# Row-block order for the last piece of the first values, early copies of half products, and two smaller moves in a two-layer hybrid trunk

## The chip, the cores and the metric

The kernel runs on one core of one Trainium2 chip. The metric is the device time of one execution in microseconds. It is the median of three runs for the kernel before, and a profile of one further execution stands beside it.

## The reference

The model has two layers of width 1024 over a sequence of 512 positions, in float32. In short:

```python
# even layer
q, k, v, g_ret, xb, g_lru = jnp.split(x @ w_in, ...)          # six blocks of 1024 columns
ret = group_norm(retention(rope(q), rope(k) * dk**-0.5, v)) * silu(g_ret)   # 8 heads of 128
lru = rg_lru_branch(xb, ...) * silu(g_lru)                    # conv, gates, scan
h = layer_norm(alpha * x + concat(ret, lru) @ w_out)
# odd layer
q, k, v, g = jnp.split(h @ w_in, ...)                         # four blocks of 2048 columns
p = softmax(mask(rope(q) @ rope(k).T)); w = p[:, :, 0] - lam * p[:, :, 1]   # two maps a head, 8 heads
o = rms_norm(w @ v) * subln_g * (1 - lambda_init)
out = layer_norm(alpha * h + (o * silu(g)) @ w_out)
```

The group norm of the retention takes the mean over a head's 128 columns away; the kernel takes it away from the values v instead, ahead of the retention, which is linear in them.

## The kernel before, in words

**Products.** Every float32 operand is split into a high and a low half (`split`, L150 to L153: a cast to the high half, L152, mostly on ScalarE; a subtraction for the low half, L153, on VectorE). A product is three matmuls, high by high, low by high and high by low (`mm3`, L157). Nearly all of TensorE's work is such groups of three matmuls with 512 columns.

**Weights.** They come in 162 pieces of 128 x 1024 floats (512 KB). `fetch` (L177) loads a piece into a raw buffer by SyncE's queue, casts it, splits it, and appends it to the ready list; `take(ahead)` hands out the next piece and fetches a given number of pieces ahead of use. In a name like w3h the number is the piece's and the letter the half; the raw buffer is w_r. At the start there are two raw buffers, later four. The first piece, w0, is loaded, cast and split in two halves of 512 columns, between the loads of x's columns (xr).

**Order.** TensorE and SyncE run in the order in which the program is written. The other engines' order is made by a scheduler from priorities (`tc.high_priority`), and instructions given to `tc.keep_in_program_order` keep the written order among themselves. Work that belongs to attention, retention and so on is interleaved with the projections by a clock of ticks (`Side`): one tick is one group of three matmuls. A job such as `attention` yields the number of ticks after which its next step is due; tables at the head of the file hold these numbers. `ATT_TURN` is, for each of the four query blocks of a head, the ticks between the transposes of the weights of the softmax (L675, split into w..h and w..l) and their product with the values (po).

**First values.** `s_unit` computes the values of the first four heads, 512 columns, for four blocks of 128 rows into four PSUM banks (ev_ps). Each of the four pieces w0 to w3 covers two of the eight slices of the contraction. In this first unit of the program the matmuls go kind by kind over the four row blocks, as the condition on `taken[0]` says; elsewhere a piece goes row block by row block. `evac` in `v_even` then takes the mean per head (vm, L459 and L460) and subtracts it (vc, L462) on VectorE, and splits the result (ev00 to ev03). The next product (gl, from piece w4) takes the first bank that comes free.

**Gates and values of the odd layer.** Groups 1 to 3 of the heads have their gate and value projections computed together in `gates_values` (gv1 to gv3), by fewer products of sums of blocks. Two products share two banks each: `one` (gv1a, two banks) and `two` (gv1b). Between the products, partial results are copied out by ScalarE (L804, p1, u and p7), since the banks go on accumulating. `product` takes two pieces, and the callback `then` runs between them. The copies of one pair of banks are issued in the callback of the product of the other pair. `load_sum` (L775) loads sums of activations that a product further on reads.

**Attention.** For a head hd and a query block qb the job does the scores of the two maps (as), the exponentials (e, L663), the combination (L671), the transposes, the product with the values (po), the root mean square (L696, then GpSimd's L699 and L367), the scaling by the gate (o, L702), two more transposes (L706) and the split into the output operand (om). The last head, 7, ends together with the last output projection (oo_ps): its sums into y (L264) and the statistics of the final layer norm (L268, L377 to L396) are on VectorE.

Of the kernel before, what the change touches and what calls it, by code (L numbers as in the profile page):

```python
# [17 lines left out]
KT = D // P  # L18
# [13 lines left out]
LN_TURN = 15  # L32
ATT_START, ATT_GAP = (12,) * 7 + (7,), (8,) * 7 + (7,)
ATT_SCORES = (7, 7, 7, 9)
ATT_TURN = (4, 3, 4, 5)
ATT_NORM = 5
ATT_VALUE, GV_VALUE = 2, 4
ATT_FREE, ATT_LENT = 2, 8
# [65 lines left out]
def trunk(ctx: ExitStack, tc: tile.TileContext, a):  # L104
# [3 lines left out]
    def pool(name, bufs, stack=ctx, **kw):  # L108
        return stack.enter_context(tc.tile_pool(name=name, bufs=bufs, **kw))
# [18 lines left out]
    def work(name):  # L128
        return wk.tile([P, S], F32, tag="wk", name=name)
# [4 lines left out]
    def bank(pl, tag, name):  # L134
        return pl.tile([P, 512], F32, tag=tag, name=name)

    def pair(pl, shape, tag, name, **kw):
        return tuple(pl.tile(shape, F32R, tag=tag + x, name=name + x, **kw) for x in "hl")
# [4 lines left out]
    def cut(t, *ix):  # L143
        return t[0][ix], t[1][ix]

    def split(src, dst, scale=None, copy=nc.scalar.copy):
        if scale is not None:
            s = sg[:, scale:scale + 1]
            nc.scalar.activation(out=dst[0], in_=src, func=AF.Identity, scale=s)
            nc.vector.scalar_tensor_tensor(out=dst[1], in0=src, scalar=s, in1=dst[0].bitcast(F32), op0=ALU.mult, op1=ALU.subtract)  # L150
            return
        copy(out=dst[0], in_=src)  # L152
        return nc.vector.tensor_tensor(out=dst[1], in0=src, in1=dst[0].bitcast(F32), op=ALU.subtract)  # L153

    def mm3(out, l, r, start, stop, kinds=range(3), **kw):
        for n in kinds:
            nc.tensor.matmul(out=out, lhsT=l[n == 2], rhs=r[n == 1], start=start and n == 0, stop=stop and n == 2, **kw)  # L157
# [30 lines left out]
    taken = [0]  # L188

    def take(ahead):  # L190
        taken[0] += 1
        while len(ready) < min(taken[0] + ahead, len(order)):
            list(fetch())
        return ready[taken[0] - 1]
# [9 lines left out]
    def s_unit(act, name, major, evac, before=None):  # L204
        def product(ps, w, sb, kt, kinds=range(3)):
            j = kt % 2 * HALF
            mm3(ps, cut(act, ALL, kt, slice(sb * P, sb * P + P)), cut(w, ALL, slice(j, j + HALF)), kt == 0, kt == KT - 1, kinds)
            if 2 in kinds:
                if kt == KT - 1:
                    evac(sb, ps)  # L210
                side.tick()

        if major:
            with tc.high_priority(P_WEIGHTS):
                ws = [take(0) for _ in range(KT // 2)]
            for sb in range(SB):
                before(sb)
                ps = bank(ps_pj, "pj", f"{name}_ps{sb}")
                for kt in range(KT):
                    product(ps, ws[kt // 2], sb, kt)  # L220
        else:
            ps = [bank(ps_pj, "pj", f"{name}_ps{sb}") for sb in range(SB)]
            for i in range(KT // 2):
                w = take(2)
                if taken[0] <= KT // 2:

                    for j in range(2):
                        for n in range(3):
                            for sb in range(SB):
                                product(ps[sb], w, sb, 2 * i + j, (n,))  # L230
                    continue
                for sb in range(SB):
                    for j in range(2):
                        product(ps[sb], w, sb, 2 * i + j)
# [39 lines left out]
    for p in range(3):  # L274
        one, two = (2 * p, 2 * p + 1)
# [5 lines left out]
    for kind, i in ev:  # L281
        if kind in ("ro", "lo", "out"):
            order += [(eo[2 * i + j + n], None) for n in {"ro": (0,), "lo": (8,), "out": (8, 0)}[kind] for j in range(2)]
        else:
            n = 4 if kind == "v" else 1
# [45 lines left out]
    for n, (lo, hi) in enumerate(((0, 1), (1, 2), (2, 4), (4, 6), (6, 8))):  # L331
        nc.sync.dma_start(out=xr[:, lo:hi], in_=a["xt"][:, lo:hi])
        if n == 0:
            next(halves)
        for kt in range(lo, hi):
            low = split(xr[:, kt], cut(x, ALL, kt))
            if n == 0:
                tc.keep_in_program_order(low)
        if n == 1:
            list(halves)  # L340
        elif 1 < n < 4:
            list(fetch())
# [66 lines left out]
    two = pool("two", 2, phase)  # L409
# [240 lines left out]
    def attention(hd, qb, q, k, m):  # L650
# [25 lines left out]
        with tc.high_priority(P_ATT):  # L676
            wt = part(n, f"w{hd}{qb}")
            split(pt[:, :n], wt)
        yield ATT_TURN[qb] + busy[0]

# [92 lines left out]
    def load_sum(n, k):  # L773
        for j in range(2):
            nc.sync.dma_start(out=sx[:, k, :, 2 * j:2 * j + 2].bitcast(F32), in_=sd[n][:, :, 2 * j:2 * j + 2])  # L775

    def silu2(x, out, t):

        nc.scalar.activation(out=t, in_=x, func=AF.Tanh, scale=0.5)
        nc.vector.scalar_tensor_tensor(out=out, in0=t, scalar=1.0, in1=x, op0=ALU.add, op1=ALU.mult)  # L780

    def gates_values(i):
        def block(r, c):
            return lambda kt, n: cut(h, ALL, 4 * c + kt, slice((2 * r + n) * P, (2 * r + n) * P + P))

        def total(k):
            return lambda kt, n: tuple(sx[:, k, x, kt, n * P:n * P + P] for x in range(2))

        def product(ps, left, start, then=lambda: None):
            for j in range(2):  # L790
                if j:
                    then()
                w = take(3)
                for n in range(2):
                    for kt in range(2 * j, 2 * j + 2):
                        c = kt % 2 * HALF
                        mm3(ps[n], left(kt, n), cut(w, ALL, slice(c, c + HALF)), start and kt == 0, kt == KT // 2 - 1, skip_group_check=not start)
                        side.tick()

        def copies(ps, name, ts):  # L800

            for n in range(2):
                ts.append(work(f"{name}{i}{n}"))
                tc.keep_in_program_order(nc.scalar.copy(out=ts[n], in_=ps[n]))  # L804

        def gate(ps, ts, r):
            g = gp.tile([P, 2, S], F32, tag="g", name=f"og{i}{r}")
            for n in range(2):
                for hd in (2 * i - 2, 2 * i - 1):
                    side.need(oj[hd, 2 * r + n])  # L810
                gates[2 * r + n, i] = g[:, n]
            for n in range(2):
                nc.vector.tensor_tensor(out=g[:, n], in0=ps[n], in1=ts[n], op=ALU.add)
                silu2(g[:, n], g[:, n], ts[n])

        busy[0] = ATT_BUSY
        one = [bank(ps_pj, "pj", f"gv{i}a{n}") for n in range(2)]
        two = [bank(ps_pj, "pj", f"gv{i}b{n}") for n in range(2)]
        p1, u, p7, low = [], [], [], []
        product(one, block(0, 0), True)  # L820
        product(two, block(0, 1), True, lambda: copies(one, "p1", p1))
        gate(two, p1, 0)
        product(one, total(0), False)

        def between():
            load_sum(0, 0)
            copies(one, "u", u)

        product(two, total(1), True, between)

        def between():
            load_sum(3, 1)
            copies(two, "p7", p7)

        product(one, total(0), False, between)
        past(i - 1)
        for n in range(2):
            nc.vector.scalar_tensor_tensor(out=p7[n], in0=one[n], scalar=-1.0, in1=p7[n], op0=ALU.mult, op1=ALU.subtract)
            low.append(pair(vp, [P, S], "v", f"ov{i}{2 + n}"))
            split(p7[n], low[n])  # L840
        product(two, block(1, 1), False)
        gate(two, u, 1)
        product(one, total(1), False)
        for n in range(2):
            t = pair(vp, [P, S], "v", f"ov{i}{n}")
            nc.scalar.activation(out=t[0], in_=one[n], func=AF.Identity, scale=-1.0)
            nc.vector.scalar_tensor_tensor(out=t[1], in0=one[n], scalar=-1.0, in1=t[0].bitcast(F32), op0=ALU.mult, op1=ALU.subtract)
            vs.setdefault(i, []).append(t)
        vs[i] += low
        vt[i] = side.now + GV_VALUE  # L850
        busy[0] = 0
# [5 lines left out]
    def past(g):  # L857
        if g >= 0:
            for hd in (2 * g, 2 * g + 1):
                for qb in range(SB):  # L860
                    side.need(oj[hd, qb])
# [25 lines left out]
    for kind, i in od:  # L887
        spare[0] = kind == "qk"
        if kind == "v":
            vs[i] = []  # L890

            def evac(sb, ps):
                past(i - 1)
                t = pair(vp, [P, S], "v", f"ov{i}{sb}")
                split(ps, t)
                vs[i].append(t)

            s_unit(h, f"ov{i}", i == 0, evac, lambda sb: side.need(hj[sb]))
            vt[i] = side.now + ATT_VALUE
            if i == 0:  # L900
# [117 lines left out]
```

## Time and profile before

| | |
|---|---|
| median of 3 runs | 927.86 us |
| lowest and highest run | 926.43 and 928.98 us |
| profiled execution | 926.57 us |
| its span | 924.8 us |
| outside the span | 1.77 us |
| granted clock of TensorE | 0.998 |
| matmuls | 4256 |

Lines of the timeline read: start in us, length in us, engine, line of the kernel, operation, output, inputs, count, and in brackets the engine's idle time ahead of it with what released it. An x4 behind a line stands for four instructions, and the length is from the first start to the last end. PE is TensorE, DVE VectorE, ACT ScalarE, POOL GpSimd, SPq the queue of SyncE.

### The profile page before, as it was taken

How to read it: one execution, taken by the hardware profiler on the slowest of the kernel's cores; microseconds unless marked ns; L12 is line 12 of the kernel's file. 1: busy time of each engine (PE TensorE's matmuls, PEld its weight loads, DVE VectorE, ACT ScalarE, POOL GpSimd, SP SyncE). 2: the span in 40 equal slices, each digit the busy share in tenths (PEclk: the TensorE clock that was granted, in tenths of full speed). 3: DMA queues.
4: the chain of work that ended last, by engine and by line, in shares of the span. 5: the costliest groups of instructions: out<-in, count | busy, mean ns of one | idle time of the engine just before them, and what ended most of it. 6: DMA issues, size and time to landing. Idle time of an engine off the chain costs nothing.

```text
span 924.8 us, 11834 instructions
## 1 busy us (share of the span) xinstructions
PE 907.2 (98%) x4256; PEld 750.4 (81%) x4256; DVE 740.8 (80%) x1223; ACT 478.3 (52%) x779; POOL 114.9 (12%) x190
## 2 busy tenths in 40 slices
PE   9899999999999999999999999999999999999996
PEld 6788887888888888888888778888888888788885
DVE  5777977967868998897888887759877679868777
ACT  5466886637565668533434456433456333655340
POOL 1311010110102010010101120000120100201022
PEclk9999999999999999999999999999999999999999
DMA  7895363782829471434941216646237392268102
GB/s 258 279 289 165 108 184 107 219 226 57 254 62 287 115 195 58 168 128 148 330 171 69 69 68 222 226 167 233 77 129 256 148 317 79 75 240 285 53 1 91
DMA packets 46522, 152.92 MB, mean 165 GB/s; under 512 B 6144, under 2 KB 6272, under 8 KB 45696
## 3 DMA queue, kind: packets, MB, share of 16 engines
q1 hardware_dynamic: 41472, 135.39, 41.5%
q0 software_dynamic: 4992, 16.78, 9.3%
q8 instruction: 33, 0.54, 0.2%
q14 instruction: 25, 0.20, 0.1%
HBM read 139.57 MB, written 37.75 MB: 192 GB/s over the span
## 4 chain that ended last, share of the span: by engine, by line
PE 84%; DVE 7%; ACT 3%; DMA 2%; issue 2%; POOL 1%; SPq 0%; DVEq 0%; ACTq 0%; POOLq 0%
PE oo_ps L157 7%; PE gr_ps L157 5%; PE out_ps L157 4%; PE q_ps L157 4%; PE gl_ps L157 4%; PE k_ps L157 4%; PE xb_ps L157 4%; PE po L157 3%; PE as L157 3%; PE gv2a L157 2%; PE ov_ps L157 2%; PE gv3a L157 2%; PE ev_ps L157 2%; PE eo_ps L157 2%; PE og_ps L157 2%; DMA w_r<-in_ev_w 2%
## 5 line engine op out<-in xcount | busy, mean ns | idle before, releaser
L663 ACT ACTIVATE e<-as,nm 128x128 f32<-128x128 f32 (+3 forms) x64 | 33.2, 523 | 61.2 <-DVE nm L660 61.1
L670 POOL TENSOR_SCALAR zr<-z 128x1 f32<-128x1 f32 x32 | 16.9, 528 | 246.9 <-ACT e L663 246.9
L702 DVE SCALAR_TENSOR_TENSOR o<-po,ars,og 128x256 f32<-128x256 f32 x32 | 15.5, 484 | 33.2 <-POOL ars L367 33.2
L185 POOL DMA_DIRECT2D t<-t x24 | 18.8, 783 | 159.3 <-DMA t<-in_od_w 155.4
L699 POOL TENSOR_SCALAR ave<-ss,zr 128x1 f32<-128x1 f32 x32 | 17.5, 548 | 145.5 <-ACT po L696 135.7
L185 POOL DMA_DIRECT2D t<-in_od_w x24 | 19.0, 793 | 118.8 <-DMA t<-in_od_w 118.7
L660 DVE CUSTOM_DVE_ANT_0 as<-as,mask 128x128 f32<-128x128 f32 (+3 forms) x64 | 30.5, 507 | 2.6 <-PE as L157 2.6
L696 ACT ACTIVATE po<-po 128x256 f32<-128x256 f32 x32 | 12.0, 374 | 27.5 <-PE po L157 27.4
L541 DVE TENSOR_TENSOR xbp<-xbp,xc 128x512 f32<-128x512 f32 x8 | 5.5, 692 | 17.5 <-ACT xbp L538 17.5
L367 POOL TENSOR_TENSOR ars<-ave,nhalf 128x1 f32<-128x1 f32 x32 | 18.8, 587 | 2.7
L671 DVE SCALAR_TENSOR_TENSOR e<-e,zr,e 128x128 f32<-128x128 f32 (+3 forms) x32 | 17.6, 549 | 0.8
L524 DVE SCALAR_TENSOR_TENSOR xc<-xbp,vecs,xc 128x509 f32<-128x509 f32 (+2 forms) x24 | 17.9, 746 | 0.2
L264 DVE TENSOR_TENSOR y<-oo_ps,y 128x512 f32<-128x512 f32 x24 | 16.1, 684 | 2.2 <-PE oo_ps L157 2.2
L367 POOL TENSOR_TENSOR lrs<-lve,nhalf 128x1 f32<-128x1 f32 x8 | 7.4, 919 | 83.1 <-DVE lve L380 83.1
L480 DVE TENSOR_TENSOR rsd<-rs,dec 128x512 f32<-128x512 f32 (+3 forms) x32 | 15.6, 487 | 2.1 <-PE rs L157 2.1
L533 ACT ACTIVATE t<-pr,vecs 128x512 f32<-128x512 f32 x8 | 5.5, 687 | 17.5 <-PE pr L157 17.4
L675 PE MATMUL wt<-ident,e 128*128 128x128 f32 x80 | 13.9, 272 | 0.0
L675 PEld LDWEIGHTS wt<-ident,e 128*128 128x128 f32 x80 | 10.5, 140 | 3.5
L706 PEld LDWEIGHTS po<-ident,o 128*128 128x128 f32 x64 | 8.8, 140 | 5.2 <-DVE o L702 1.3
L706 PE MATMUL po<-ident,o 128*128 128x128 f32 x64 | 12.3, 274 | 0.4 <-DVE o L702 0.4
L152 ACT CAST hh<-ht 128x512 fp32r<-128x512 f32 x8 | 4.7, 587 | 15.3 <-PE ht L620 15.3
L668 DVE RECIPROCAL zr<-z 128x1 f32<-128x1 f32 x32 | 5.2, 162 | 9.2 <-ACT e L663 9.2
(2801 smaller groups left out, 3463.9 us busy)
## 6 DMA issues: line engine op xcount, KB each, us to landing
w_r<-in_od_w SPq DMA_DIRECT2D x58, 512.0 KB, 5.6
w_r<-in_ev_w SPq DMA_DIRECT2D x47, 512.0 KB, 5.6
t<-in_od_w SPq DMA_DIRECT2D x48, 256.0 KB, 5.8
sx<-sd SPq DMA_DIRECT2D x24, 512.0 KB, 5.9
w_r<-t SPq DMA_DIRECT2D x24, 512.0 KB, 3.3
w_r<-in_ev_wo SPq DMA_DIRECT2D x16, 512.0 KB, 4.6
w_r<-in_od_wo SPq DMA_DIRECT2D x16, 512.0 KB, 4.2
t<-in_od_w POOLq DMA_DIRECT2D x24, 256.0 KB, 5.4
```

The costliest lines, as they stand in the source:

```text
L157: nc.tensor.matmul(out=out, lhsT=l[n == 2], rhs=r[n == 1], start=start and n == 0, stop=stop and n == 2, **kw)
L185: nc.gpsimd.dma_start(out=dst, in_=two, max_dma_last_dim=4 * D, accum_op=ALU.add)
L264: nc.vector.tensor_tensor(out=yy, in0=ps, in1=yy, op=ALU.add)
L367: nc.gpsimd.tensor_tensor(out=out, in0=var, in1=nhalf[:, :1], op=ALU.pow)
L524: nc.vector.scalar_tensor_tensor(out=xc[:, sh:], in0=xb[:, :S - sh], scalar=conv_w(w, c), in1=xc[:, sh:], op0=ALU.mult, op1=ALU.add)
L660: nc.vector.tensor_tensor_reduce(out=ps[:, :n], in0=ps[:, :n], in1=mask[:, S - n:], scale=-QK_SCALE, scalar=3.0e38, op0=ALU.add, op1=ALU.m ...
L663: nc.scalar.activation(out=e, in_=ps[:, :n], func=AF.Exp, scale=-1.0, bias=nm, accum_out=z[:, mp:mp + 1])
L670: nc.gpsimd.tensor_scalar(out=zr[:, 1:2], in0=z[:, 0:1], scalar1=z[:, 0:1], scalar2=EPS, op0=ALU.mult, op1=ALU.mult)
L671: nc.vector.scalar_tensor_tensor(out=ee[0], in0=ee[1], scalar=zr[:, 0:1], in1=ee[0], op0=ALU.mult, op1=ALU.add)
L675: nc.tensor.transpose(out=pt[:, kb * P:kb * P + P], in_=ee[0][:, kb * P:kb * P + P], identity=ident)
L699: nc.gpsimd.tensor_scalar(out=ve, in0=ss, scalar1=zr[:, 1:2], scalar2=None, op0=ALU.add)
L706: nc.tensor.transpose(out=pm[:, i * P:i * P + P], in_=o[:, i * P:i * P + P], identity=ident)
```

## The change

Four edits. In the first values the fourth piece, w3, goes row block by row block (`<` in place of `<=`): six matmuls for block 0, then six for block 1, and so on. In `gates_values` the copies of p1, u and p7 are issued right behind the product whose banks they read, ahead of the next product, and no longer in the callback in the midst of it; the loads of sums stay in the callbacks. The last number of `ATT_TURN`, for query block 3, is 4 in place of 5. At the start, w0's second half is loaded, cast and split right behind its first, ahead of x's second column.

```diff
-ATT_TURN = (4, 3, 4, 5)
+ATT_TURN = (4, 3, 4, 4)
...
-                if taken[0] <= KT // 2:
+                if taken[0] < KT // 2:
...
-        if n == 1:
+        if n == 0:
             list(halves)
...
         product(one, block(0, 0), True)
-        product(two, block(0, 1), True, lambda: copies(one, "p1", p1))
+        copies(one, "p1", p1)
+        product(two, block(0, 1), True)
         gate(two, p1, 0)
         product(one, total(0), False)
-
-        def between():
-            load_sum(0, 0)
-            copies(one, "u", u)
-
-        product(two, total(1), True, between)
-
-        def between():
-            load_sum(3, 1)
-            copies(two, "p7", p7)
-
-        product(one, total(0), False, between)
+        copies(one, "u", u)
+        product(two, total(1), True, lambda: load_sum(0, 0))
+        copies(two, "p7", p7)
+        product(one, total(0), False, lambda: load_sum(3, 1))
         past(i - 1)
```

Lines behind L820 stand seven lines higher in the changed kernel.

The first place is VectorE at the end of the first values. The banks ev_ps_246 to ev_ps_249 are those of row blocks 0 to 3, w5l and w6l are splits of weight pieces, and gw0l is the split of a gate's weights.

```order
 L153 TENSOR_TENSOR w5l<-w_r,w5h 128x1024
-L153 TENSOR_TENSOR w6l<-w_r,w6h 128x1024
 L459 TENSOR_REDUCE vm<-ev_ps_246 128x4
 L459 TENSOR_REDUCE vm<-ev_ps_247 128x4
 L460 TENSOR_SCALAR vm<-vm 128x4
+L153 TENSOR_TENSOR w6l<-w_r,w6h 128x1024
+L462 TENSOR_TENSOR vc<-ev_ps_246,vm 128x512
+L460 TENSOR_SCALAR vm<-vm 128x4
 L153 TENSOR_TENSOR gw0l<-gw_437,gw0h 128x512
-L460 TENSOR_SCALAR vm<-vm 128x4
-L462 TENSOR_TENSOR vc<-ev_ps_246,vm 128x512
 L462 TENSOR_TENSOR vc<-ev_ps_247,vm 128x512
```

The reductions of blocks 0 and 1 now stand ahead of w6's split, and block 0's subtraction stands right behind it, ahead of gw0's.

The second place is ScalarE in the first of the gate and value units. The names p_ are the copies p1 of the banks gv1a, e_ are exponentials of the next head's first query block, and w90h and w91h are casts of weight pieces.

```order
 L152 CAST w90h<-w_r 128x1024
 L696 ACTIVATE po_4993,ss<-po_4993 128x256
+L804 COPY p_5011<-gv1a_4913 128x512
+L804 COPY p_5013<-gv1a_4914 128x512
 L152 CAST w91h<-w_r 128x1024
-L663 ACTIVATE e_5036,z<-as_5030,nm 128x128
-L663 ACTIVATE e_5044,z<-as_5038,nm 128x128
-L804 COPY p_5051<-gv1a_4913 128x512
+L663 ACTIVATE e_5040,z<-as_5034,nm 128x128
+L663 ACTIVATE e_5048,z<-as_5042,nm 128x128
 L152 CAST om1h<-po_4993 128x2x128
-L804 COPY p_5053<-gv1a_4914 128x512
```

Both copies now stand ahead of w91's cast and of the exponentials; before, one stood behind the exponentials and the other behind a further cast.

The third place is VectorE near the end of the program, around the output o of head 7's last query block. The rows L264 are sums of an output projection's bank into y, L268 the statistics of a half row.

```order
 L396 SCALAR_TENSOR_TENSOR y<-y,lrs,ln_8324 128x512
+L702 SCALAR_TENSOR_TENSOR o_8460<-po_8441,ars,og_7721 128x256
 L264 TENSOR_TENSOR y<-oo_ps_8415,y 128x512
 L268 BN_STATS bst<-y 128x6
-L702 SCALAR_TENSOR_TENSOR o_8463<-po_8444,ars,og_7721 128x256
 L264 TENSOR_TENSOR y<-oo_ps_8416,y 128x512
 L268 BN_STATS bst<-y 128x6
 L377 BN_AGGR bmv<-bst 128x2
```

The scaling o now stands ahead of a sum and its statistics that stood ahead of it before.

## The prediction

> **What bounds the kernel now.** I read the summary of engines first, then the waits of TensorE, then the timeline around each wait, then the chain that ended last.
>
> ```profile
> span 924.8 us, 11834 instructions
> PE 907.2 (98%) x4256; PEld 750.4 (81%) x4256; DVE 740.8 (80%) x1223; ACT 478.3 (52%) x779; POOL 114.9 (12%) x190
> PE 84%; DVE 7%; ACT 3%; DMA 2%; issue 2%; POOL 1%; SPq 0%; DVEq 0%; ACTq 0%; POOLq 0%
> ```
>
> TensorE is busy for 907.2 of 924.8 us, and the chain is 84% its own work. The change takes no matmul away, so a gain can only come out of the 17.6 us in which TensorE does nothing, and the chain's other 16% is mostly the start and the tail. The waits of TensorE (line waited for: us in total, times, longest) say which holes have an owner:
>
> ```profile
> PE gl_ps L157 <- DVE vc L462: 2.6, 1, 2.6
> ...
> PE gv1a L157 <- ACT p L804: 0.7, 1, 0.7
> PE po L157 <- ACT w03h L152: 0.5, 1, 0.5
> ...
> PE po L157 <- DVE w11l L153: 0.5, 1, 0.5
> ...
> PE po L157 <- DVE w03l L153: 0.4, 1, 0.4
> ...
> PE gv3a L157 <- ACT p L804: 0.3, 1, 0.3
> PE gv2a L157 <- ACT p L804: 0.3, 1, 0.3
> PE gv1b L157 <- DVE om1l L153: 0.3, 1, 0.3
> ```
>
> Three of the edits touch these: the first values the first row, the copies the three gv*a rows, and the earlier value product the rows of po and, through what follows it, om1l. Outside these, TensorE runs without a hole of note, so what it gains early it carries to the end, unless a later wait eats it.
>
> **First values by row blocks.** The timeline around the longest wait:
>
> ```profile
> 21.39 0.33 SPq L177 DMA_DIRECT2D w_r<-in_ev_w  x1
> 23.53 1.23 DVE L153 TENSOR_TENSOR w5l<-w_r,w5h 128x1024 fp32r<-128x1024 f32 x1
> 26.53 1.05 ACT L152 CAST w6h<-w_r 128x1024 fp32r<-128x1024 f32 x1 [3.04 <-DMA w_r<-in_ev_w]
> 27.62 1.23 DVE L153 TENSOR_TENSOR w6l<-w_r,w6h 128x1024 fp32r<-128x1024 f32 x1 [2.87 <-ACT w6h L152]
> 27.87 1.07 PE L157 MATMUL ev_ps<-w3h,xl 128*128 128x512 f32 x4
> 28.76 1.28 DVE L459 TENSOR_REDUCE vm<-ev_ps 128x4 f32<-128x512 f32 x2
> 30.70 1.28 DVE L462 TENSOR_TENSOR vc<-ev_ps,vm 128x512 f32<-128x512 f32 x2
> 31.53 0.47 PE L157 MATMUL gl_ps<-xh,w4h 128*128 128x512 f32 x1 [2.59 <-DVE vc L462]
> 37.22 5.44 PE xb_ps L157 x24
> ```
>
> A chain row gives the pace: 24 matmuls in 5.44 us, 0.227 us each. So TensorE is through with the values at 27.87 + 4 x 0.227 = 28.78, and the next product starts at 31.53: 2.75 us lost, because all four banks finish together, VectorE reduces after w6l, and the first bank comes free only with the first vc (half of the 1.28 us row, 30.70 + 0.64). With the fourth piece by blocks, 24 matmuls a block by piece are 6: block 0 is done 18 matmuls (4.1 us) before the end, at 24.7, block 1 at 26.1. Their two reductions fit behind w5l (24.76), in time that VectorE spends idle (2.87 us before w6l). The new order of VectorE then has w6l between the reductions and block 0's vc. That decides the size. If w6 lands as it does now, w6l ends at 28.85, vc at 29.5, and the product starts at 29.57: gain 1.96. If it lands 0.72 us or more sooner, vc is done when TensorE arrives: gain 2.75, or 2.83 with a refill. It should land sooner: w6's load (issued at 21.39) waits for w3's split to give a raw buffer back, w3's own load stands behind w2's in the queue, and w2 takes the buffer of w0's halves, which the last part below lets go sooner. I take **-2.6** (nearer to the upper end, for the reason just given) and keep -1.96 to -2.83. What VectorE does behind that is the same work as now.
>
> [...] The load of w6 takes 26.53 - 21.39 = 5.1 us from issue to cast. [...]
>
> **Copies right behind their product.** Before, ScalarE's given order put the two copies of a product behind a piece's cast and two exponentials. The rows of the three places:
>
> ```profile
> 548.23 0.39 ACT L696 ACTIVATE po<-po 128x256 f32<-128x256 f32 x1
> 549.54 1.05 ACT L152 CAST w91h<-w_r 128x1024 fp32r<-128x1024 f32 x1 [0.81 <-PE gv1b L157]
> 553.22 0.40 PE L157 MATMUL gv1b<-w87h,hl 128*128 128x512 f32 x1
> 553.72 0.57 ACT L804 COPY p<-gv1a 128x512 f32<-128x512 f32 x1
> 554.35 0.51 PE L157 MATMUL gv1a<-w88h,sx 128*128 128x512 f32 x1 [0.73 <-ACT p L804]
> 554.69 0.40 PE L157 MATMUL gv1a<-w88l,sx 128*128 128x512 f32 x1
> ...
> 678.12 0.40 PE L157 MATMUL gv2b<-w113h,hl 128*128 128x512 f32 x1
> 678.82 0.50 PE L157 MATMUL gv2a<-w114h,sx 128*128 128x512 f32 x1 [0.30 <-ACT p L804]
> ```
>
> The product whose bank is copied ended some 8 us earlier, so the copies can stand anywhere after. In the new order they come behind po's square (548.23) and ahead of w91h, in the 0.81 us in which ScalarE waits; they last about 0.6 each, so w91h begins about 0.4 us later, and w91 is used in a product two pieces on: hidden. Slots lost now: 554.35 - 553.45 = 0.90 (553.22 + one matmul), 678.82 - 678.35 = 0.47, and the third place has the same 0.30 wait and so about the same 0.47. Restarting also costs 554.69 - 554.35 = 0.34 in place of 0.227, 0.1 each, 0.3. Sum **-2.1**; bounds -1.3 (the three waits alone, 0.73 + 0.30 + 0.30) and -2.24. The copies of u and p7 move in the same way; TensorE waits for neither now, and what they push back by some 1.2 us (the cast of w95) has room of the same kind: 0. The two sums that SP loads between halves stay at their places on SP.
>
> **A value product one tick sooner.** Block 3 of a head has its product 3 matmuls (0.68 us) sooner after its transposes. The order moves it at heads 0, 1, 3, 5, 6 and 7; at 2 and 4 it stands where it stood.
>
> ```profile
> 520.73 0.57 ACT L152 CAST w03h<-wt 128x512 fp32r<-128x512 f32 x1
> 521.35 0.38 PE L157 MATMUL po<-ov00h,w03h 128*128 128x256 f32 x1 [0.55 <-ACT w03h L152]
> 522.23 0.39 PE L157 MATMUL po<-ov00h,w03l 128*128 128x256 f32 x1 [0.38 <-DVE w03l L153]
> ```
>
> At head 0 TensorE already waits 0.55 and 0.38 us for w03's halves, and they don't come sooner for being wanted sooner: the three matmuls that stood ahead of the product now stand behind it, and the waits grow by 0.68. Against that, block 3's output leaves 0.68 us sooner, and VectorE's order puts it ahead of a rotary sum and the next scores' masks ahead of a split; the two later waits (w11l 0.5, om1l 0.3 in the table) hang on that row of work. With both gone their slots (0.6 and 0.4) pay the 0.68 back and more. Bounds -0.35 to +0.68; I take 0, since each end has one good reason. At heads 1, 3, 5 and 6 no wait stands in the table: 0.
>
> At head 7 the end is set by VectorE:
>
> ```profile
> 903.21 0.69 DVE L264 TENSOR_TENSOR y<-oo_ps,y 128x512 f32<-128x512 f32 x1
> 903.94 0.69 DVE L268 BATCH_NORM_STATS2 bst<-y 128x6 f32<-128x512 f32 x1
> 905.79 0.48 DVE L702 SCALAR_TENSOR_TENSOR o<-po,ars,og 128x256 f32<-128x256 f32 x1 [1.16 <-POOL ars L367]
> 906.19 0.68 DVE L264 TENSOR_TENSOR y<-oo_ps,y 128x512 f32<-128x512 f32 x1
> ```
>
> Now a sum and its statistics (903.21 to 904.63) fill time in which VectorE would wait for o. In the new order o stands ahead of them: o comes 0.68 sooner, at 905.11, and 1.37 us of work that was done ahead of it follows it. From o on, the chain that ended last is the layer norm's own work on VectorE and GpSimd, so the end moves by 1.37 - 0.68 = +0.69; neighbours overlap by 0.08 (906.19 against 905.79 + 0.48), and there are two or three more of these. I take **+0.5**; bounds 0 (if a later idle stretch of the norm swallows it) and +0.7.
>
> **w0's halves in a row.** The half of w0 now lands ahead of x's second column.
>
> ```profile
> 8.11 0.62 ACT L152 CAST w0h<-w_r 128x512 fp32r<-128x512 f32 x1 [1.70 <-DMA w_r<-in_ev_w]
> 8.78 1.19 PE L157 MATMUL ev_ps<-w0h,xh 128*128 128x512 f32 x4 [0.26 <-ACT w0h L152]
> 9.48 0.33 SPq L177 DMA_DIRECT2D w_r<-in_ev_w  x1
> ```
>
> TensorE's second column waits for the later of the two loads, cast by ScalarE in 0.62 us; the two are of like size and only change places, so it starts at 8.78 either way: 0, bounds -0.3 to +0.3 (its wait of 0.26 now). What does change is that w0's raw buffer is done sooner: w2's load (9.48) waits for the last split of w0, which can now end about 7.2, and the loads behind move up with it, to the benefit of the first part.
>
> Sum: -2.6 - 2.1 + 0 + 0.5 + 0 = **-4.2**. The profiled execution took 926.57 (924.8 and 1.77 around it), which would become 922.4; the median of the runs is 1.29 above it, 927.86, and becomes **923.7**.
>
> **The rivals.** First: w6's split takes the place of the reductions as what ends last, and head 0's 0.68 isn't won back. VectorE works its rows in order, so vc can't pass w6l while w6's load is late; for it speaks that the new order has just that, against it that w6's load follows w3l, which should come sooner. -1.96 - 2.1 + 0.68 + 0.5 = -2.9: 925.0. [...]
>
> Second: the copies' gain comes back as a wait of the next value product. In the gates' new order a tanh of ScalarE stands ahead of the cast of the block-3 weights (w13h), and a product of VectorE ahead of their split (w13l), while the product itself comes 0.9 and 0.68 us sooner.
>
> ```profile
> 555.57 0.69 DVE L153 TENSOR_TENSOR w13l<-wt,w13h 128x512 fp32r<-128x512 f32 x1
> 558.25 0.28 PE L157 MATMUL po<-ov00h,w13l 128*128 128x256 f32 x1
> ```
>
> Wanted at 558.25 - 1.0 - 0.68 = 556.6, ready now at 556.26, and some 0.3 us later by the two rows put ahead: even. If it is late by the whole slot at all three stages, that term is 0 and the sum -2.1 (-2.6 + 0.5): 925.8.
>
> Third, slower: all six moved products arrive ahead of their weights' low half, each losing up to its 0.68 (4.1), with the tail's 0.5, the copies' gain eaten and the first part only at -1.96: +2.6, 930.5. It decides from the point where the split of block 3's weights ends later than the product's third matmul; at head 1 that is even, at the others no wait in the table speaks for it.
>
> That the change doesn't do what it says holds for heads 2 and 4 (no move), and costs nothing.
>
> **How the numbers follow.** Forecast 0.70; first rival 0.17, second 0.09, third 0.04. Two executions of this kernel differ by up to 0.3%, 2.78 us, so faster means below 925.1. The forecast's own bounds are -1.96 - 1.3 + 0.68 + 0.7 + 0.3 = -1.6 and -2.83 - 2.24 - 0.35 + 0 - 0.3 = -5.7; that is 926.3 and 922.1. I give 921.9 to 926.3, with 0.2 below for the spread of a median; it also holds the first two rivals. Faster: 0.65 of the forecast's 0.70 and half of the first rival, 0.73; same: the rest of these and the second rival, 0.23; slower 0.04.
>
> **What the profile after would show.** Right: the wait of gl_ps for vc is under 0.7 us, with w6h's cast before 25.9; the waits of gv1a, gv2a and gv3a for L804 are gone and w13l has none over 0.3; at head 0 po's waits for w03h and w03l sum to about 1.6, and those for w11l and om1l are gone; o of head 7 stands ahead of two sums, and the time from it to the end is about 1.2 us longer. Wrong: a wait of gl_ps of 0.8 or more (first rival), waits of po for w13l, w33l or w53l near 0.9 (second), or for the low half of block 3's weights at the other heads (third); and a weight piece that TensorE waits for in the first 50 us would show that the new order of loads costs what I took for nothing.

## The result, and the profile after

The changed kernel takes 922.15 us (median of 5 runs, 921.5 to 924.02) against 927.86 us before: a ratio of 0.9944, with a 95% interval of 0.9927 to 0.9961. Between the two profiled executions the time fell from 926.57 to 922.15, by 4.4 us, where 4.2 was forecast; the medians differ by 5.7. One thing must be known to read these numbers: about half of the executions of the kernel before (11 of 22 in the first group below, by their mean clock of 0.995 to 0.997) took some 1.6 us longer than the others at 0.998, to which the profiled one belongs; the experiments below put this down to a granted clock of about half that TensorE had for some 3.4 us behind its longest wait.

The profile after, its span and its engines, and TensorE's waits:

```profile
span 920.4 us, 11834 instructions
PE 906.0 (98%) x4256; PEld 750.0 (81%) x4256; DVE 739.8 (80%) x1223; ACT 477.9 (52%) x779; POOL 115.5 (13%) x190
```

```profile
PE po L157 <- ACT w03h L152: 1.3, 1, 1.3
...
PE out_ps L157 <- DVE gl L450: 0.8, 1, 0.8
...
PE po L157 <- DVE w03l L153: 0.4, 1, 0.4
```

The 2.6 us wait of gl_ps is gone, and so are the waits of gv1a, gv2a and gv3a for the copies, of po for w11l and of gv1b for om1l. The wait for w03h has grown from 0.5 to 1.3, and that of out_ps for gl, which was 0.3, to 0.8. The place of the first values in the timeline:

```profile
23.00 1.05 ACT L152 CAST w6h<-w_r 128x1024 fp32r<-128x1024 f32 x1 [0.80 <-DMA w_r<-in_ev_w]
...
24.75 0.69 DVE L459 TENSOR_REDUCE vm<-ev_ps 128x4 f32<-128x512 f32 x1 [1.30 <-PE ev_ps L157]
...
26.78 1.22 DVE L153 TENSOR_TENSOR w6l<-w_r,w6h 128x1024 fp32r<-128x1024 f32 x1
...
27.92 0.69 DVE L462 TENSOR_TENSOR vc<-ev_ps,vm 128x512 f32<-128x512 f32 x1
...
28.75 0.47 PE L157 MATMUL gl_ps<-xh,w4h 128*128 128x512 f32 x1
```

Block 0's reduction starts at 24.75, its vc is done at 28.61, and gl_ps starts at 28.75 with no wait: 2.78 us sooner than before. At the first gate and value unit the two copies stand together, done 3.7 us ahead of need, and w13l is ready at 553.47 for a matmul at 553.71:

```profile
545.90 1.07 ACT L804 COPY p<-gv1a 128x512 f32<-128x512 f32 x2
...
550.72 0.40 PE L157 MATMUL gv1a<-w88h,sx 128*128 128x512 f32 x1
...
552.79 0.68 DVE L153 TENSOR_TENSOR w13l<-wt,w13h 128x512 fp32r<-128x512 f32 x1
...
553.71 0.28 PE L157 MATMUL po<-ov00h,w13l 128*128 128x256 f32 x1
```

Head 0's value product, and the chain from head 7's o to the end (start, length, what; DVEq L1007 is the end of the program):

```profile
519.09 0.38 PE L157 MATMUL po<-ov00h,w03h 128*128 128x256 f32 x1 [1.25 <-ACT w03h L152]
...
519.96 0.38 PE L157 MATMUL po<-ov00h,w03l 128*128 128x256 f32 x1 [0.37 <-DVE w03l L153]
```

```profile
900.51 0.48 DVE o L702
900.99 0.61 DVE y L264
...
916.73 0.66 DVEq L1007
```

Before, the same last piece of the chain stood here:

```profile
921.12 0.66 DVEq L1014
```

From o to that piece it was 921.12 - 905.79 = 15.33 us before and is 916.73 - 900.51 = 16.22 now: 0.89 longer.

### The profile page after: what moved, and what is told of

Same layout as the page of the kernel before. It is cut to its first block, busy times and chain, and to the rows that moved or that the text cites. A ratio compares the mean times of both kernels' runs of the same rounds, so it can differ in the third digit from the quotient of the medians.

```text
span 920.4 us, 11834 instructions
## 1 busy us (share of the span) xinstructions
PE 906.0 (98%) x4256; PEld 750.0 (81%) x4256; DVE 739.8 (80%) x1223; ACT 477.9 (52%) x779; POOL 115.5 (13%) x190
## 4 chain that ended last, share of the span: by engine, by line
PE 82%; DVE 8%; ACT 4%; DMA 2%; issue 2%; POOL 2%; SPq 0%; DVEq 0%; ACTq 0%; POOLq 0%
PE oo_ps L157 7%; PE out_ps L157 4%; PE gr_ps L157 4%; PE ev_ps L157 4%; PE gl_ps L157 4%; PE q_ps L157 3%; PE xb_ps L157 3%; PE k_ps L157 3%; PE po L157 3%; PE ov_ps L157 2%; PE as L157 2%; PE gv1a L157 2%; PE eo_ps L157 2%; PE og_ps L157 2%; PE gv2a L157 2%
## 5 line engine op out<-in xcount | busy, mean ns | idle before, releaser
L264 DVE TENSOR_TENSOR y<-oo_ps,y 128x512 f32<-128x512 f32 x24 | 16.0, 685 | 2.2 <-PE oo_ps L157 2.1
L663 ACT ACTIVATION_READ_ACCUMULATOR e<-as,nm 128x1 f32 x64 | 12.5, 195 | 0.0
```

The source lines that it names most:

```text
L264: nc.vector.tensor_tensor(out=yy, in0=ps, in1=yy, op=ALU.add)
L663: nc.scalar.activation(out=e, in_=ps[:, :n], func=AF.Exp, scale=-1.0, bias=nm, accum_out=z[:, mp:mp + 1])
```

## The experiments

The theory after the result: the four parts give what their slots give in the profile, and the rest of the medians' difference is a clock that no longer falls. The rival: a part is worth more than its slots. The first four kernels each take one part alone, beside 22 runs of the kernel before (median 927.42); each ratio below is against the runs of the kernel before that were taken beside it (25 for the second group of kernels, median 927.96; 23 for the third, 927.86).

**Rows alone.**

```diff
-                if taken[0] <= KT // 2:
+                if taken[0] < KT // 2:
```

> The kernel before with the row-block order of the fourth piece alone. My theory: the size of this part hangs on when w6's low half is split, and that on the order of the first loads. Without the new order of w0's halves w6h's cast stands at about 26.5 us as before, w6l ends near 28.9, the first vc near 29.5, and gl_ps starts at 29.5 to 29.6 with a wait of 0.7 to 0.8 us: 2.0 us sooner than before, time about -2.0. Rival: the row order alone does it all, gl_ps starts at 28.8 without a wait and the time falls by 2.75 us. A second question: in the changed kernel 0.48 us of the gain was given back at the wait of out_ps for gl near 140 us. If what gives it back is a fixed price of TensorE being sooner, the wait grows here too (to 0.6 or more from 0.34); if it was one late load, it stays at 0.34.

924.66 us, ratio 0.9965 (0.9952 to 0.9978). The rival was right on the wait:

```profile
25.78 1.05 ACT L152 CAST w6h<-w_r 128x1024 fp32r<-128x1024 f32 x1 [2.60 <-DVE vm L459]
...
28.24 0.69 DVE L462 TENSOR_TENSOR vc<-ev_ps,vm 128x512 f32<-128x512 f32 x1
...
29.08 0.47 PE L157 MATMUL gl_ps<-xh,w4h 128*128 128x512 f32 x1
```

vc ends at 28.93 and TensorE comes to gl_ps with no wait named; it starts at 29.08 because the first values themselves ran later here (a wait of 1.15 for w1h at 12.13). The bracket of w6h's cast names vm, whose reduction had just ended; its load was issued at 21.1, and the loads of its kind issued here between 18 and 32 us took 4.5 to 5.2 us to land, so it is more likely the load that the cast waited for. The cast ended at 26.83, 0.28 us before VectorE came to w6l behind the two reductions (27.11). So the row order doesn't need the new order of loads in this execution, with little to spare: of the seven profiles without the new load order, five have w6h's cast at 26.3 to 27.0, 0.5 to 1.2 us later than here (another has it at 24.07). The runs speak more for the theory: all five have a clock of 0.997 or 0.998, and their median is 1.9 below the 926.53 of those runs of the kernel before that have 0.998, which is nearer to the theory's 2.0 than to the rival's 2.75. Whether a late load took part of the gain in the executions without a profile is not settled. The wait of out_ps for gl stayed at 0.35.

**Copies alone.** The edit is the last part of the diff above.

> The kernel before with the early copies alone. Theory: the waits of gv1a, gv2a and gv3a for the copies (L804) go, the slots of 0.90, 0.47 and 0.47 us with them and about 0.1 each of restart; time -1.8 to -2.1. Rival: the products behind them arrive ahead of their weights' low halves (w13l, w33l, w53l) or the gates' products push something else, new waits of po of 0.4 or more each, and the time falls by under 1.0.

924.85 us, ratio 0.9968 (0.9956 to 0.9981); no wait for L804 is left, nor one for w13l, w33l or w53l. Its runs at a mean clock of 0.997 or 0.998 took 923.81 to 925.05, those of the kernel before at 0.998 took 925.72 to 927.12: about 1.8 us. Its profile showed what the one of before had not. The stretch behind the wait of gl_ps, by a table of windows, and a pair of matmuls there. A row of the table has the stretch and its length; the busy time and, in brackets, the instructions of PE, of PE's loading of weights, of DVE, ACT and POOL; then the granted clock, the busy share of the DMA engines and GB/s.

```profile
28.00:32.00 4.00, 1.02 (x6) 0.55 (x5) 4.00 (x8) 1.87 (x3) 3.06 (x3) 1.00 0.93 366
32.00:36.00 4.00, 4.00 (x11) 3.14 (x12) 4.00 (x10) 2.57 (x4) 0.77 (x1) 0.59 0.96 213
```

```profile
31.91 0.47 PE L157 MATMUL gl_ps<-xh,w4h 128*128 128x512 f32 x1 [2.98 <-DVE vc L462]
...
35.19 0.63 PE L157 MATMUL gl_ps<-xh,w4h 128*128 128x512 f32 x1
35.62 0.63 PE L157 MATMUL gl_ps<-xl,w4h 128*128 128x512 f32 x1
```

Matmuls follow each other at 0.43 us in place of 0.227 from 32.7 to 36.0; the next unit starts at 39.09, 7.18 us after gl_ps and not 5.52 as in the kernel before.

**The value product alone.**

```diff
-ATT_TURN = (4, 3, 4, 5)
+ATT_TURN = (4, 3, 4, 4)
```

> The kernel before with the last number of ATT_TURN at 4 alone. Theory: at head 0 the wait for w03h grows from 0.55 to about 1.25 (+0.7), the later waits for w11l (0.46) and om1l (0.26) go (slots 0.6 and 0.4, and 0.2 of order), and the tail from head 7's o to the end grows by 0.9 while o is 0.68 sooner (+0.2): net -0.2, so no difference that the runs can tell. Rival: the six earlier products each wait for their weights, +1.5 to +4.6.

928.22 us, ratio 1.0008 (0.9996 to 1.002). Both of the small items are there, w11l and om1l wait no more; but 10 runs spread from 925.87 to 931.17. In the profile, of the run of 931.17 at a mean clock of 0.992, the clock falls behind head 0's product:

```profile
524.70 0.39 PE L157 MATMUL po<-ov00h,w03h 128*128 128x256 f32 x1 [1.23 <-ACT w03h L152]
...
525.57 0.39 PE L157 MATMUL po<-ov00h,w03l 128*128 128x256 f32 x1 [0.37 <-DVE w03l L153]
```

```profile
526.00:528.00 2.00, 2.00 (x11) 1.90 (x10) 1.97 (x4) 0.40 (x2) 0.00 (x0) 0.55 0.00 0
528.00:530.00 2.00, 2.00 (x7) 1.52 (x7) 1.33 (x2) 0.08 (x1) 1.75 (x2) 0.59 0.00 0
530.00:532.00 2.00, 2.00 (x13) 1.74 (x12) 1.79 (x6) 0.90 (x3) 0.18 (x1) 1.00 0.74 236
```

By the table's 0.55 and 0.59 these four microseconds lost 0.90 + 0.82 = 1.7 us, some 3.4 us at half the clock. The run lies 4.5 to 5.3 us above the three at 0.998 (925.87 to 926.66), so by estimate it had the low clock elsewhere too, most likely behind gl_ps. A longer wait at head 0 thus had a price that no slot of the profile before shows: behind two waits of 1.23 and 0.37 us the clock was low for 3.4 us.

**w0's halves alone.**

```diff
-        if n == 1:
+        if n == 0:
             list(halves)
```

> The kernel before with w0's halves loaded in a row alone. Theory: w6h's cast comes 2 to 3.5 us sooner (near 23 to 24.5 in place of 26.5), but the four banks still end together at 28.8, so gl_ps starts at 31.4 to 31.5 and the time stays (-0.1 to 0). Rival: the order of the loads is itself worth a gain: gl_ps 0.5 us or more sooner.

927.64 us, ratio 1.0 (0.9991 to 1.001). The loads move as forecast, and the time stays, though gl_ps comes 0.5 sooner, as the rival had it:

```profile
24.27 1.06 ACT L152 CAST w6h<-w_r 128x1024 fp32r<-128x1024 f32 x1 [0.22 <-DMA w_r<-in_ev_w]
...
31.04 0.47 PE L157 MATMUL gl_ps<-xh,w4h 128*128 128x512 f32 x1 [2.13 <-DVE vc L462]
```

```profile
143.98 0.51 PE L157 MATMUL out_ps<-w21h,lrum0h 128*128 128x512 f32 x1 [0.96 <-DVE gl L450]
```

out_ps waits 0.6 more than before and takes it back.

The next four ask whether it is TensorE's idleness that brings the clock down, and what head 0's and head 7's products are worth. In the kernel before, of the 22 runs named, 11 had a mean clock of 0.998 and took 925.72 to 927.12, and 11 had 0.995 to 0.997 and took 927.71 to 928.52: two groups, some 1.6 us apart.

**The wait filled.** Put behind the first values of the kernel before (the constants' products go to a bank that nothing reads):

```diff
             v = v_even(i)
+            if i == 0:
+                for _ in range(11):
+                    busy_pe(4)
```

> The kernel before, with 11 warm-up matmuls (2.5 us, on constants, into the idle bank) put where TensorE waits for gl_ps's bank. Nothing waits less: gl_ps still starts at about 31.5 to 32. Theory: half of the executions of the kernel before lose about 1.7 us more than the profiled one, because the granted clock falls to half for some 3.4 us behind that wait; with TensorE busy in the wait the clock stays, no run stands at 0.996 or below, and the median is 926.5 (-1 us). Rival: the low clock has nothing to do with the wait, and the runs fall in two groups as before, median 927.4.

926.8 us, 11 runs, all within 926.57 and 927.17; ratio 0.999 (0.9982 to 0.9999). gl_ps starts at 31.66, as late as ever, and the second group of runs is gone; the median is 1.2 below that of the 25 runs beside it:

```profile
28.00:32.00 4.00, 4.00 (x19) 3.31 (x18) 3.94 (x9) 2.34 (x4) 3.48 (x7) 1.00 0.95 378
32.00:36.00 4.00, 4.00 (x20) 3.30 (x19) 4.00 (x9) 2.45 (x4) 0.77 (x1) 1.00 1.06 230
```

**The changed kernel without its third part.**

```diff
-ATT_TURN = (4, 3, 4, 4)
+ATT_TURN = (4, 3, 4, 5)
```

> The changed kernel with the last number of ATT_TURN back at 5. Theory: the wait for w03h goes back from 1.25 to 0.55, and with it the cases in which the clock falls behind it; the waits for w11l and om1l come back (slots 0.6 and 0.4), and the tail from o to the end shrinks by 0.9 while o is 0.68 later. By the slots alone +0.1, by the clock -0.8 on the mean: the undisturbed runs stay at 921.5 to 922.5 and none stands near 924. Rival: the runs near 924 of the changed kernel come from elsewhere and stay.

922.62 us, 5 runs within 921.95 and 922.73. The changed kernel's own runs were 921.5, 921.84 and 922.15, and 923.98 and 924.02 at a mean clock of 0.995 and 0.996. So the two near 924 seem to go with the earlier product (2 of 5 runs against 0 of 5 show it only weakly; the filled wait below adds to it), and without them the product at 4 is by these few runs, taken at different times, some 0.5 us better than at 5. out_ps waited 0.97 for gl in this profile, 0.14 more than in the changed kernel's.

**Head 0's product later.**

```diff
-        yield ATT_TURN[qb] + busy[0]
+        yield ATT_TURN[qb] + busy[0] + (3 if (hd, qb) == (0, 3) else 0)
```

> The changed kernel with the value product of head 0's block 3 three ticks later than in it (7 in place of 4; the others stay at 4). Theory: TensorE no longer waits for w03h and w03l (slots 1.5 and 0.6 us), 1.5 to 2 us less, and the clock doesn't fall there: 920 to 920.7 and no run near 924. Rival: what follows head 0's block 3 is late in its place (the output operand for the next products, scores of head 1): new waits of the same sum, 921.5 to 922.

925.6 us, ratio 0.9975 (0.9966 to 0.9984): 3.4 us slower than the changed kernel; the theory fell. w03h and w03l are waited for no more, but the whole queue of attention's steps behind it changed. The rival had named new waits, but of no larger sum than the old ones. TensorE's waits are now:

```profile
PE po L706 <- DVE o L702: 1.7, 3, 1.3
...
PE wt L675 <- DVE e L671: 1.4, 2, 1.1
...
PE po L157 <- DVE om1l L153: 1.0, 1, 1.0
PE po L157 <- DVE w11l L153: 0.8, 1, 0.8
```

Single waits of 1.1 to 1.3 us stand in this kernel, and its mean clock was 0.997 or 0.998 in ten of its eleven runs (the eleventh took 1840.87 us, at 1.0).

**Head 7's product back, besides.**

```diff
-        yield ATT_TURN[qb] + busy[0]
+        yield ATT_TURN[qb] + busy[0] + {(0, 3): 3, (7, 3): 1}.get((hd, qb), 0)
```

> As the one before it, and head 7's block 3 back at 5. Theory: the tail from o to the end is 0.9 shorter and o 0.68 later: 0.2 us less than the one before it. Rival: the tail's order is worth nothing by itself, 0 to +0.1.

925.13 us, ratio 0.9977 (0.9967 to 0.9988). From o to the last piece of the chain it is 919.73 - 904.39 = 15.34 us, against 920.36 - 904.13 = 16.23 in the one before it: 0.89 again. The end is 0.63 sooner, of which 0.40 had been there since the start of the program: the tail's part is 0.2.

The last four: can the clock be held at head 0, how short a wait still brings it down, and which of the copies count.

**Head 0's wait filled.** In the changed kernel, ahead of the product:

```diff
+        if (hd, qb) == (0, 3):
+            for _ in range(10):
+                nc.tensor.matmul(out=po[:, 2 * P:], lhsT=ones, rhs=ones.unsqueeze(1).to_broadcast([P, 2, P]), start=True, stop=True)
         for kb in range(qb + 1):
```

> The changed kernel with 10 small matmuls on constants (1.2 us, 256 columns each, into the unused half of po's bank) ahead of the value product of head 0's block 3, where TensorE otherwise waits 1.25 us for w03h. Theory: the wait's length stays in the time, but the clock doesn't fall behind it: no run at a clock of 0.996 or less, all of them at 921.5 to 922.5, median 921.8. Rival: the runs near 924 of the changed kernel have another cause and stay, or the matmuls delay the product and cost 0.3 or more.

922.41 us, 6 runs from 921.98 to 923.56, all at a clock of 0.997 or 0.998; ratio 0.9944 (0.9929 to 0.9958). No run has the low clock, but the theory's median of 921.8 was missed by 0.6, and no gain over the changed kernel's median can be told. In the profile gv1b waited for om1l again (0.26), 0.4 us that the changed kernel had saved; the rival's cost of the added matmuls (0.3 or more) is not excluded.

**That, and head 7's product back.**

```diff
-        yield ATT_TURN[qb] + busy[0]
+        yield ATT_TURN[qb] + busy[0] + ((hd, qb) == (7, 3))
```

> As the one before it, and head 7's block 3 one tick later, as in the kernel before. Theory: the tail's order goes back and the end comes 0.2 us sooner than in the one before it (the two kernels with head 0's product late differed by 0.5 in this). Rival: no difference.

922.34 us, 6 runs from 921.93 to 922.66; ratio 0.9942 (0.9929 to 0.9954). It is steady, but not clearly faster than the changed kernel. The tail's 0.2 is in it: the end is 0.30 sooner than in the one before it, of which 0.05 was there at w87.

**Half the filling**, in the kernel before: 5 in place of 11.

> The kernel before with 5 warm-up matmuls (1.1 us) at the head of the wait for gl_ps's bank, so that TensorE is idle for about 1.5 us in place of 2.6. Theory: the clock falls more seldom the shorter the idle time is: fewer runs at 0.996 or less than the half of the kernel before, perhaps none (the changed kernel's 1.25 and 0.37 us at head 0 did it in 2 of 5). Rival: any idle time above 1 us does it as often as before.

926.73 us, ratio 0.9989 (0.998 to 0.9998), 12 runs, one of them at a clock of 0.996 (928.85). TensorE was idle here for

```profile
PE gl_ps L157 <- DVE vc L462: 1.0, 1, 1.0
```

so idle time of 1.0 us behind busy matmuls brought the clock down in 1 of these 12 runs at most. With the waits of 2.1 to 3.0 that the profiles show for the kernels that keep the wait whole, 11 of the first 22 runs of the kernel before had the low clock by their mean clock and time, 6 of 10 with w0's halves alone, 1 of 6 with the copies and 3 of 10 with the first copies (below).

**The first copies alone**, in the kernel before; u and p7 stay where they were.

```diff
-        product(two, block(0, 1), True, lambda: copies(one, "p1", p1))
+        copies(one, "p1", p1)
+        product(two, block(0, 1), True)
```

> The kernel before with the copies of p1 alone moved right behind their product; u and p7 stay in the midst of the next. Theory: the whole gain of the copies' part sits here: the three waits for L804 go, 1.8 to 2 us less in the undisturbed runs (924.5 to 925). Rival: the copies of u and p7 carry a part, and this gives less than 1.3.

924.72 us, ratio 0.9971 (0.9961 to 0.9982); no wait for L804 is left. Its profiled end is 919.45, 1.67 us ahead of the profile before, to the copies' 1.9 in the changed kernel: the gain sits in p1, and u and p7 are worth some 0.2 at most.

## Why the prediction was right

The start times of the same matmuls in the two profiles give each term (after minus before, at the first matmul of gl_ps, of the pieces named, and at the end):

| term | forecast | measured |
|---|---|---|
| first values | -2.6 | -2.78 at gl_ps, of which 0.5 was given back at out_ps |
| copies | -2.1 | -2.2 (0.91, 0.47, 0.45 and 0.1 each of restart), 0.3 given back ahead of w139: -1.9 |
| head 0 | 0 | 0.0 up to gv1a (-2.28 at w82, -2.29 at w84), then -0.4 where om1l had been waited for |
| head 7 | +0.5 | +0.2 |
| w0's halves | 0 | 0 by themselves |
| sum | -4.2 | -4.4 |

The runs bear the sum out too. The medians of the parts alone, taken over the runs at 0.997 or 0.998, lie below the 926.53 of the kernel before at 0.998 by 1.87 (rows), 1.76 (copies), 0.49 (value product, three runs at 0.998) and 0.09 (halves, four runs at 0.998), together 4.2. So the rival, that a part is worth more than its slots, has nothing to explain beyond the clock.

The first values came out near the upper end, but the reason that was given for it is only half shown. The prediction held that w6's load had to come 0.72 us sooner than 26.53, or 0.8 us of the gain would be lost, and that the new order of loads would see to it. The load did come sooner (w6h's cast at 23.0 to 24.3 in the profiles with the new order, at 24.1 to 27.0, mostly above 26, in those without). But the rows alone met the condition without it, by a hair (25.78), and had no wait. The prediction took the landing from one execution as if it were the kernel's; it differs by up to 2.9 us from one to the next. No profile has the row order and a late load together, so the first rival's price was not seen, and what the new order of loads adds to the row order stays open.

w0's halves cost nothing, as forecast, though not in the way that the prediction had it: TensorE waits 0.4 to 1.5 us for xh, the cast of x's columns, in six of the seven profiles with the new order and in none without, but on the whole less for w0 and w1, and the first values end at 28.6 to 29.3 against 28.8 to 29.2.

The copies' term held, and the second rival didn't come: w13l had 0.24 us left, where the working had found it even. At head 0 the wait grew by 0.70, as forecast, and the two later waits paid it back: the zero was a sum of these, and om1l's slot came on top, outside the stated bound by a hair. The third rival had no place: the other heads' products found their weights ready.

The tail's step was right in kind and too large: 1.37 us of work did move behind o, and o to end grew by 0.89, not by 1.2; from o up to the step L394 behind the statistics it took 1.47 longer, but the split om7l, which had stood between two steps of the norm for 0.33, now stands in a pause, and the next two sums and their statistics take 2.51 in place of 2.76.

What the prediction didn't see is the clock. It set the sum against the profiled execution, and added the 1.29 us between that and the median as if this were the same in both kernels. It is not: about half of the runs before had the low clock, which the filled wait of gl_ps took away; the changed kernel has no such wait, and this gave the medians another 1.3 us (the filled wait alone gave 1.2). So the median came 1.5 us below the 923.7 that was forecast. That it still fell inside the range, 0.25 above the lower end, is in part luck, since the range has no term for these 1.3 us. The 25 runs of the kernel before beside the second group of kernels lie between 926.14 and 930.49, 0.5% apart, where the prediction took 0.3%. The changed kernel bought a risk of the same kind at head 0 (2 of its 5 runs, at 0.995 and 0.996, near 924).

Not settled is the wait of out_ps for gl. Its cause in the profile after is one load that came later than ScalarE wanted it, with all that ScalarE had queued behind it:

```profile
116.44 1.06 ACT L152 CAST w22h<-w_r 128x1024 fp32r<-128x1024 f32 x1 [0.78 <-DMA w_r<-in_ev_wo]
```

The wait was 0.83 to 0.97 in three of the seven profiles with the new order of loads, and 0.34 to 0.42 in the other four and in all seven without it. In all fourteen it goes with this cast, which waited 0.78 to 0.93 for its load in the three, 0.38 where out_ps waited 0.42, and not at all in the others. Whether that order makes the late landing likelier, 80 us further on, stays open.

## What to carry to other kernels

A profiled execution is one draw: set it beside the runs' spread, and if the runs fall into two groups, find out which group it belongs to before the sum is made against it. A long wait of TensorE cost more than its length here: 2.6 us and, in about half of the executions, 1.6 us more for the slow matmuls behind it; constants multiplied in the wait showed this (11 runs within 0.6 us, and none of the second group). Putting off one step of a crowded queue to spare a wait moved every step behind it (head 0's product three ticks later: 3.4 us slower), so look for the waits that such a step makes.

## What the runs showed of the hardware

After 2.1 to 3.0 us without a matmul the granted clock fell to about half in about half of the executions (by the runs' clocks and times from 1 of 6 with the copies alone to 6 of 10 with w0's halves alone). Where a profile shows it, with the copies alone, matmuls followed each other at 0.43 us in place of 0.227 from 32.7 to 36.0, 3.3 us, at a granted clock of 0.59 over the window from 32 to 36. Two waits of 1.23 and 0.37 us with two small matmuls between them did it too, in the profile of the value product alone (0.55 and 0.59 over two windows of 2 us, some 3.4 us at half) and, by the runs' clocks, in 2 of 5 executions of the changed kernel. A wait of 1.0 did it once in 12 at most (half the filling), and single ones of 1.1 to 1.3 in none of ten (head 0's product later). With the wait of gl_ps filled the clock was 0.997 or 0.998 in all 11 runs.

Rows that were ready stood behind rows that were not, in the order given, as the prediction's first rival had it of VectorE. In the kernel before ScalarE was idle for 0.81, 1.48 and 0.83 us ahead of w91's cast and of two exponentials, and the first copy of gv1a, whose last matmul had ended at 545.15, came behind them at 553.72. In the changed kernel VectorE was idle for 1.82 us ahead of head 7's o at 900.51, and the sum behind it, whose bank was done at 899.55, started at 900.91.
